# A hybrid decoder layer on one core: a softplus series cut into background pieces, and the mixer's four products in another order

## The chip, the cores and the metric

One core of a Trainium2 chip runs the whole layer. The time is the device time of one execution in microseconds (us). Three runs of the kernel before gave 1193.51, 1194.63 and 1196.12 us, so the median is 1194.63.

## The reference

One layer has three sub-layers on 512 tokens with 1024 channels, in float32. Each one scales and shifts its input by columns that come from a conditioning vector c, adds its result to the residual and normalises. The parts that the change touches are those of the middle sub-layer (`lam` is `rglru_lambda`):

```python
mod = silu(c) @ ada_w + ada_b                  # 9 columns of 1024
u = modulate(x, sh2, sc2)
xr, gr, conf_in, gate_a, gate_b = split(u @ w_in)
xr = causal_depthwise_conv(xr, rnn_conv_w, rnn_conv_b)       # 4 taps
log_a = -8 * softplus(-lam) * sigmoid(xr @ w_r + b_r)        # per head
h  = scan(exp(log_a), sqrt(-expm1(2 * log_a)) * (sigmoid(xr @ w_i + b_i) * xr))
ya = (h * gelu(gr)) @ rnn_w_proj
hb = causal_depthwise_conv(glu(conf_in), conf_dw_w, conf_dw_b)   # 31 taps
yb = silu(layer_norm(hb, conf_ln_g, conf_ln_b)) @ conf_w_proj
out = (sigmoid(gate_a) * ya + sigmoid(gate_b) * yb) @ mix_w_out
```

The first and the third sub-layer are SwiGLU networks with 22 blocks of 128 hidden channels.

## The kernel before

All activations stay in SBUF, channels on the partitions and the 512 tokens along the row; X is the residual. Every product is done in three passes, so that float32 accuracy is kept with a narrower type: an operand is split into a high part (`hi`, a copy into fp32r on ScalarE) and a low part (`lo`, the subtraction, line 145). Weights come in slabs of two blocks of 128 columns (`raw`), and are split in the same way into whi (ScalarE, line 141) and wlo (line 145, on VectorE, or on POOL where `lo_engine` says so). Activations for a product lie in U (Uh, Ul) or in H (Hh, Hl). One block of 128 output channels is a unit: 24 matmuls, 8 chunks of the contraction by 3 passes (lines 240 to 242), into one of six PSUM banks. In the second part of the FFN's contraction a unit has 6 chunks, so 18 matmuls.

The order of work is the order in which the program is written, engine by engine, and each engine works in that order. Three helpers put work between units. `unit()` opens a time slot; weights are split up to four (high) and three (low) units ahead. `defer(n, f)` runs f in the n-th slot from now. `later(cost, f)` puts f in a queue, and `background()`, called twice in a unit, takes pieces from it as long as their costs fit a budget per unit. `until(condition)` holds that queue back until the condition is true. The 31 taps of the depthwise convolution (line 841) are such background work in the mixer, one instruction on VectorE each, and so are the 56 ada sums (line 257) in the first FFN.

The first FFN goes by three parts of hidden blocks: g and u products, h = silu(g) * u, the split of h into H, then eight y products, which add to X (line 714). `early` is called behind the first part's g and u products (`gcol` in `ffn`). It issues the softplus series (lines 939 to 953), which gives the columns sp and nsp for the RG-LRU, and one column for the residual (line 288).

The mixer goes through glu and xr, gr products, with the RG-LRU of each pair of channel blocks deferred behind them; its last step writes the pair's result into H (line 992 and its splits). Then come eight units each of ga, ya, gb and yb. ga and gb read U, ya reads H. `conv_norm` queues the norm over the channels of the convolution's output CV: its sum over the pairs (lc_sum, line 866), a fold of two halves (876), the mean by a matmul (lc_mu, 880), centring (888), squares on ScalarE (890) and their sums (894), the token sums by matmuls (lc_tok, 317), the deviation's power on POOL (334), its diagonal (lc_dg, 341) and broadcast (lc_rs, 908), scaling (914), silu, and the splits into H behind `until(free)`, which is true once the ya products are issued. yb reads H then, and the merged result goes into U.

## Time and profile before

The profiled execution took 1194.8 us, of which 1193.0 us are the span from the first to the last instruction.

| what | value |
|---|---|
| times of three runs | 1193.51, 1194.63, 1196.12 us |
| profiled execution, its span | 1194.8, 1193.0 us |
| mean granted TensorE clock | 0.988 |
| TensorE matmuls, busy | 1159.4 us, 97% |
| VectorE, busy | 747.3 us, 63% |
| ScalarE, busy | 436.6 us, 37% |
| POOL (GpSimd), busy | 215.6 us, 18% |
| DMA | 151.64 MB |

How to read it: PE is TensorE, PEld its weight loads, DVE VectorE, ACT ScalarE, POOL GpSimd, SP the engine that issues the DMAs. A timeline row has the start in us from the span's start, the duration (of several alike, from the first start to the last end), engine, line, operation, output <- inputs, shapes and count; in brackets stands how long the engine was idle before it and what ended the wait. The granted clock is a share of the full 2.4 GHz. Matmuls overlap, so the time of one is the distance from its start to the next one's, and not its duration.

### The profile page before, as it was taken

How to read it: one execution, taken by the hardware profiler on the slowest of the kernel's cores; microseconds unless marked ns; L12 is line 12 of the kernel's file. 1: busy time of each engine (PE TensorE's matmuls, PEld its weight loads, DVE VectorE, ACT ScalarE, POOL GpSimd, SP SyncE). 2: the span in 40 equal slices, each digit the busy share in tenths (PEclk: the TensorE clock that was granted, in tenths of full speed). 3: DMA queues.
4: the chain of work that ended last, by engine and by line, in shares of the span. 5: the costliest groups of instructions: out<-in, count | busy, mean ns of one | idle time of the engine just before them, and what ended most of it. 6: DMA issues, size and time to landing. Idle time of an engine off the chain costs nothing.

```text
span 1193.0 us, 13555 instructions
## 1 busy us (share of the span) xinstructions
PE 1159.4 (97%) x5527; PEld 973.6 (82%) x5527; DVE 747.3 (63%) x1030; ACT 436.6 (37%) x559; POOL 215.6 (18%) x112
## 2 busy tenths in 40 slices
PE   7998999999999999998998999999999999999996
PEld 5887888888889988887787878889888888888886
DVE  7877776733349596998999744587423332433266
ACT  4533222223223625576653372326422122222222
POOL 3200000000003455353536340021400000000002
PEclk9998999999999999998999999999999999999998
DMA  9785766522222122322223212221322222322202
GB/s 372 268 344 207 292 240 230 226 106 105 74 104 107 47 104 80 106 94 78 94 106 116 79 57 102 106 106 36 109 104 107 106 72 79 132 99 79 106 36 71
DMA packets 30318, 151.64 MB, mean 127 GB/s; under 512 B 3376, under 2 KB 5424, under 8 KB 18480
## 3 DMA queue, kind: packets, MB, share of 16 engines
q1 hardware_dynamic: 30256, 150.78, 34.5%
q8 instruction: 43, 0.70, 0.2%
q14 instruction: 19, 0.16, 0.0%
HBM read 148.67 MB, written 2.10 MB: 126 GB/s over the span
## 4 chain that ended last, share of the span: by engine, by line
PE 76%; DVE 15%; issue 4%; ACT 3%; POOL 1%; DMA 1%; SPq 0%; POOLq 0%; ACTq 0%; DVEq 0%
PE g L240 6%; PE u L240 6%; PE u L242 6%; PE g L242 6%; PE g L241 6%; PE u L241 6%; DVE cv L841 6%; PE y L241 6%; PE y L242 6%; PE y L240 6%; PE st L759 4%; DVE i L988 1%; PE yb L240 1%; PE yb L242 1%; PE yb L241 1%
## 5 line engine op out<-in xcount | busy, mean ns | idle before, releaser
L145 POOL TENSOR_TENSOR wlo<-raw,whi 128x1024 fp32r<-128x1024 f32 (+1 forms) x69 | 169.1, 2465 | 568.9 <-ACT whi L141 568.9
L141 ACT CAST whi<-raw 128x1024 fp32r<-128x1024 f32 (+2 forms) x204 | 205.4, 1021 | 165.1 <-DMA raw<-in_wide 124.9
L841 DVE SCALAR_TENSOR_TENSOR cv<-glu,prm,cv 128x511 f32<-128x511 f32 (+14 forms) x240 | 159.4, 728 | 12.5 <-ACT cv L821 12.5
L145 DVE TENSOR_TENSOR wlo<-raw,whi 128x1024 fp32r<-128x1024 f32 (+1 forms) x135 | 158.3, 1191 | 9.2 <-ACT whi L141 9.0
L689 DVE TENSOR_TENSOR h<-u,h 128x512 f32<-128x512 f32 x38 | 26.3, 691 | 205.7 <-PE u L242 205.7
L240 PE MATMUL g<-Uh,whi 128*128 128x512 f32 x304 | 118.3, 389 | 0.0
L241 PE MATMUL g<-Ul,whi 128*128 128x512 f32 x304 | 118.3, 389 | 0.0
L242 PE MATMUL g<-Uh,wlo 128*128 128x512 f32 x304 | 118.3, 389 | 0.0
L240 PE MATMUL u<-Uh,whi 128*128 128x512 f32 x304 | 118.3, 389 | 0.0
L241 PE MATMUL u<-Ul,whi 128*128 128x512 f32 x304 | 118.3, 389 | 0.0
L242 PE MATMUL u<-Uh,wlo 128*128 128x512 f32 x304 | 118.3, 389 | 0.0
L241 PE MATMUL y<-Hl,whi 128*128 128x512 f32 x288 | 113.3, 393 | 3.8 <-DVE Hl L145 3.8
L242 PE MATMUL y<-Hh,wlo 128*128 128x512 f32 x288 | 113.0, 392 | 0.0
L240 PE MATMUL y<-Hh,whi 128*128 128x512 f32 x288 | 113.0, 392 | 0.0
L141 ACT CAST Hh<-h 128x512 fp32r<-128x512 f32 x44 | 27.0, 620 | 178.9 <-DVE h L689 178.9
L257 DVE SCALAR_TENSOR_TENSOR ada<-ada,silu_c 128x1024 f32<-128x1024 f32 x72 | 86.6, 1224 | 5.1 <-DMA ada<-in_ada 5.1
L334 POOL TENSOR_TENSOR l_y<-l_va,half 128x2 f32<-128x2 f32 x5 | 3.5, 708 | 359.1 <-DVE l_va L333 359.1
L241 PEld LDWEIGHTS y<-Hl,whi 128*128 128x128 f32 x288 | 54.7, 190 | 15.7 <-DVE Hl L145 4.2
L242 PEld LDWEIGHTS g<-Uh,wlo 128*128 128x128 f32 x304 | 57.1, 188 | 12.0
L241 PEld LDWEIGHTS u<-Ul,whi 128*128 128x128 f32 x304 | 57.1, 188 | 11.9
L242 PEld LDWEIGHTS u<-Uh,wlo 128*128 128x128 f32 x304 | 57.1, 188 | 11.8
L241 PEld LDWEIGHTS g<-Ul,whi 128*128 128x128 f32 x304 | 57.0, 188 | 11.8
(273 smaller groups left out, 2353.7 us busy)
## 6 DMA issues: line engine op xcount, KB each, us to landing
raw<-in_wide SPq DMA_DIRECT2D x92, 1024.0 KB, 4.8
ada<-in_ada SPq DMA_DIRECT2D x72, 512.0 KB, 7.4
raw<-in_six SPq DMA_DIRECT2D x8, 768.0 KB, 4.2
straw<-in_start SPq DMA_DIRECT2D x8, 512.0 KB, 8.8
X<-in_xT SPq DMA_DIRECT2D x8, 256.0 KB, 9.0
out_y<-X SPq DMA_DIRECT2D x8, 256.0 KB, 2.2
raw<-in_rg SPq DMA_DIRECT2D x4, 256.0 KB, 2.7
silu_c<-in_c SPq DMA_DIRECT2D x1, 512.0 KB, 3.9
```

The lines of the kernel that those rows point to most:

```text
L141: self.nc.scalar.copy(out=out, in_=src)
L145: (engine or self.nc.vector).tensor_tensor(out=out, in0=src, in1=hi.bitcast(F32), op=ALU.subtract)
L240: t.matmul(ps, lhsT=w[0], rhs=x[0], start=first, stop=False)
L241: t.matmul(ps, lhsT=w[0], rhs=x[1], start=False, stop=False)
L242: t.matmul(ps, lhsT=w[1], rhs=x[0], start=False, stop=last)
L257: self.nc.vector.scalar_tensor_tensor(out=raw, in0=raw, scalar=1.0, in1=self.sc, op0=ALU.mult, op1=ALU.mult, accum_out=self.mod[:, j : j + 1])
L334: self.nc.gpsimd.tensor_tensor(out=y, in0=va, in1=self.half[:, :nb], op=ALU.pow)
L689: self.nc.vector.tensor_tensor(out=h, in0=pu, in1=h, op=ALU.mult)
L759: nc.tensor.matmul(ps[i], lhsT=w[k][a][:, i * P : (i + 1) * P], rhs=self.U[b][:, k, :], start=k == 0 and (a, b) == (0, 0), stop=k == KC - ...
L841: self.nc.vector.scalar_tensor_tensor(out=acc[:, n:], in0=glu[:, : T - n], scalar=self.col("conf_dw_w", c, NTAP - 1 - n), in1=acc[:, n:], ...
L988: v.tensor_tensor_scan(out=i_[:, j, :], data0=r[:, j, :], data1=xc[:, j, :], initial=0.0, op0=ALU.mult, op1=ALU.add)
```

## The change

The softplus series is issued after the ada queue, as background pieces: `begin`, `ratio`, eight `term`s and `end`, with costs of 1.0, 1.0, 0.5 each and 1.0. `early` is gone; at its place only the residual's column is computed. In the mixer all sixteen gate products (bank name gate) come first, then ya, then yb, and the slabs of weights lie in that order. The norm's splits write U and not H, and are free once the gate products are issued; yb reads U, the merged result goes to H, and what follows the mixer reads H.

```diff
--- before.py
+++ after.py
@@ -918,9 +918,9 @@
                 nc.scalar.activation(out=x, in_=x, func=AF.Silu, scale=self.col("conf_ln_g", m), bias=self.col("conf_ln_b", m))
 
         def split(p):
-            hi = self.H[0][:, 2 * p : 2 * p + 2, :]
+            hi = self.U[0][:, 2 * p : 2 * p + 2, :]
             self.hi(hi, CV[p])
-            return lambda: self.lo(self.H[1][:, 2 * p : 2 * p + 2, :], CV[p], hi)
+            return lambda: self.lo(self.U[1][:, 2 * p : 2 * p + 2, :], CV[p], hi)
 
         ends = []
         for p in range(4):
@@ -933,24 +933,38 @@
 
     def softplus_cols(self):
 
+
         v, s = self.nc.vector, self.nc.scalar
         lam = self.vec("rglru_lambda")
         sp, nsp, e, z, z2, q = (self.new_drv() for _ in range(6))
-        s.activation(out=e, in_=lam, func=AF.Abs)
-        s.activation(out=e, in_=e, func=AF.Exp, scale=-1.0)
-        v.tensor_scalar(out=z2, in0=e, scalar1=2.0, scalar2=None, op0=ALU.add)
-        v.reciprocal(out=z2, in_=z2)
-        v.tensor_tensor(out=z, in0=e, in1=z2, op=ALU.mult)
-        v.tensor_tensor(out=z2, in0=z, in1=z, op=ALU.mult)
-        v.memset(q, 1.0 / 17)
-        for n in range(15, 0, -2):
+
+        def begin():
+            s.activation(out=e, in_=lam, func=AF.Abs)
+            s.activation(out=e, in_=e, func=AF.Exp, scale=-1.0)
+            v.memset(q, 1.0 / 17)
+
+        def ratio():
+            v.tensor_scalar(out=z2, in0=e, scalar1=2.0, scalar2=None, op0=ALU.add)
+            v.reciprocal(out=z2, in_=z2)
+            v.tensor_tensor(out=z, in0=e, in1=z2, op=ALU.mult)
+            v.tensor_tensor(out=z2, in0=z, in1=z, op=ALU.mult)
+
+        def term(n):
             v.tensor_tensor(out=q, in0=q, in1=z2, op=ALU.mult)
             v.tensor_scalar(out=q, in0=q, scalar1=1.0 / n, scalar2=None, op0=ALU.add)
-        v.scalar_tensor_tensor(out=q, in0=q, scalar=2.0, in1=z, op0=ALU.mult, op1=ALU.mult)
-        v.tensor_scalar(out=z, in0=lam, scalar1=-1.0, scalar2=0.0, op0=ALU.mult, op1=ALU.max)
-        v.tensor_tensor(out=q, in0=q, in1=z, op=ALU.add)
-        v.tensor_scalar(out=sp, in0=q, scalar1=8.0, scalar2=None, op0=ALU.mult)
-        v.tensor_scalar(out=nsp, in0=q, scalar1=-8.0, scalar2=None, op0=ALU.mult)
+
+        def end():
+            v.scalar_tensor_tensor(out=q, in0=q, scalar=2.0, in1=z, op0=ALU.mult, op1=ALU.mult)
+            v.tensor_scalar(out=z, in0=lam, scalar1=-1.0, scalar2=0.0, op0=ALU.mult, op1=ALU.max)
+            v.tensor_tensor(out=q, in0=q, in1=z, op=ALU.add)
+            v.tensor_scalar(out=sp, in0=q, scalar1=8.0, scalar2=None, op0=ALU.mult)
+            v.tensor_scalar(out=nsp, in0=q, scalar1=-8.0, scalar2=None, op0=ALU.mult)
+
+        self.later(1.0, begin)
+        self.later(1.0, ratio)
+        for n in range(15, 0, -2):
+            self.later(0.5, lambda n=n: term(n))
+        self.later(1.0, end)
         return sp, nsp
 
     def rglru(self, mp, xc, gg, rg, sp, nsp):
@@ -1050,49 +1064,45 @@
             for j in range(2):
                 s.activation(out=gg[:, j, :], in_=pg[j], func=AF.Gelu_apprx_tanh)
             self.defer(2, lambda mp=mp, xc=xc, gg=gg, w=self.take(): self.rglru(mp, xc, gg, w, sp, nsp))
-        ya_done = [False]
-        self.conv_norm(lambda: ya_done[0])
+        gates_done = [False]
+        self.conv_norm(lambda: gates_done[0])
 
         self.budget = 4.8
-        ma = [self.pair(f"ma{p}") for p in range(4)]
-        for m in range(KC):
-            ps = self.bank("ga")
-            self.group(ps, self.unit(), self.U)
-            s.activation(out=ma[m // 2][:, m % 2, :], in_=ps, func=AF.Sigmoid)
+        both = []
+        for name in ("ma", "sb"):
+            gates = [self.pair(f"{name}{p}") for p in range(4)]
+            both.append(gates)
+            for m in range(KC):
+                ps = self.bank("gate")
+                self.group(ps, self.unit(), self.U)
+                s.activation(out=gates[m // 2][:, m % 2, :], in_=ps, func=AF.Sigmoid)
+        ma, sb = both
+        gates_done[0] = True
         for m in range(KC):
             ps = self.bank("ya")
             self.group(ps, self.unit(), self.H)
             t = ma[m // 2][:, m % 2, :]
             v.tensor_tensor(out=t, in0=ps, in1=t, op=ALU.mult)
-        ya_done[0] = True
-        sb = [self.pair(f"sb{p}") for p in range(4)]
-        for m in range(KC):
-            ps = self.bank("gb")
-            self.group(ps, self.unit(), self.U)
-            s.activation(out=sb[m // 2][:, m % 2, :], in_=ps, func=AF.Sigmoid)
         self.drain()
         self.lo_engine = nc.vector
         for m in range(KC):
             ps = self.bank("yb")
-            self.group(ps, self.unit(), self.H)
+            self.group(ps, self.unit(), self.U)
             t = sb[m // 2][:, m % 2, :]
             v.tensor_tensor(out=t, in0=ps, in1=t, op=ALU.mult)
             v.tensor_tensor(out=t, in0=t, in1=ma[m // 2][:, m % 2, :], op=ALU.add)
-            hi = self.U[0][:, m, :]
+            hi = self.H[0][:, m, :]
             self.hi(hi, t)
-            self.defer(1, lambda m=m, t=t, hi=hi: self.lo(self.U[1][:, m, :], t, hi))
-        self.ln_front("l2", self.U, g)
+            self.defer(1, lambda m=m, t=t, hi=hi: self.lo(self.H[1][:, m, :], t, hi))
+        self.ln_front("l2", self.H, g)
 
     def run(self):
         nc, d, X = self.nc, self.d, self.X
-        def early():
-            self.softplus = self.softplus_cols()
-            return self.gate_col(G1, 0.5)
-
         self.startup()
         self.ada_queue()
+        self.softplus = self.softplus_cols()
         self.budget = 2.0
-        g1 = self.ffn("l1", 4, early)
+        g1 = self.ffn("l1", 4, lambda: self.gate_col(G1, 0.5))
         self.drain()
         c2 = self.affine_cols("ln1_g", "ln1_b", SC2, SH2)
         hb = self.boundary("l1", self.H, g1, c2)
@@ -1100,7 +1110,7 @@
         self.mixer(hb, g2, c2)
         c3 = self.affine_cols("ln2_g", "ln2_b", SC3, SH3)
         self.budget = 0.0
-        hb = self.boundary("l2", self.U, g2, c3)
+        hb = self.boundary("l2", self.H, g2, c3)
         ends = [self.swiglu(hb[2 * i], hb[2 * i + 1], i) for i in range(2)]
         for e in ends:
             e()
@@ -1162,8 +1172,8 @@
         order.append(("rg", mp, [4 * P]))
         rg.append(np.concatenate([w[2 * mp + j] for w in (wr, wi) for j in range(2)], axis=1))
     both(ga)
+    both(gb)
     both(i["rnn_w_proj"])
-    both(gb)
     both(i["conf_w_proj"])
     both(i["mix_w_out"])
     ffn(2, 0)
```

The first place is VectorE at the end of the first part of the first FFN, where h is the last hidden block, drv are the small columns, and Hl is the low part of that block, which the y products read. Before:

```order
L689 TENSOR_TENSOR h_776<-u,h_776 128x512
L941 TENSOR_SCALAR drv<-drv 128x8
L942 RECIPROCAL drv<-drv 128x8
...
L952 TENSOR_SCALAR drv<-drv 128x8
L953 TENSOR_SCALAR drv<-drv 128x8
L288 TENSOR_SCALAR drv<-mod 128x8
L145 TENSOR_TENSOR Hl<-h_776,Hh 128x512
```

and now:

```order
L689 TENSOR_TENSOR h_776<-u,h_776 128x512
L288 TENSOR_SCALAR drv<-mod 128x8
L145 TENSOR_TENSOR Hl<-h_776,Hh 128x512
```

The 26 instructions of the series no longer stand between h and Hl. They now stand among the y products of the second part, on the same engine (X<-y adds a product to the residual):

```order
L278 TENSOR_TENSOR mod<-mod,prm 128x8
L944 MEMSET drv 128x8
L714 SCALAR_TENSOR_TENSOR X<-y,drv,X 128x512
L145 TENSOR_TENSOR wlo_1684<-raw_1566,whi_1651 128x768
L947 TENSOR_SCALAR drv<-drv 128x8
L948 RECIPROCAL drv<-drv 128x8
...
L954 TENSOR_SCALAR drv<-drv 128x8
L714 SCALAR_TENSOR_TENSOR X<-y,drv,X 128x512
```

The rest follows behind the next two additions to X, eight and eleven instructions at a time.

The second place is TensorE in the mixer, from the last ga product to the first yb product. Before:

```order
L242 MATMUL ga<-Uh,wlo_4443 128x512
L240 MATMUL ya<-Hh,whi_4441 128x512
...
L242 MATMUL ya<-Hh,wlo_4761 128x512
L240 MATMUL gb<-Uh,whi_4759 128x512
...
L880 MATMUL lc_mu<-lc_sum,inv_d 128x512
...
L242 MATMUL gb<-Uh,wlo_5060 128x512
L240 MATMUL yb<-Hh,whi_5058 128x512
```

and now:

```order
L242 MATMUL gate<-Uh,wlo_4443 128x512
L240 MATMUL gate<-Uh,whi_4441 128x512
...
L242 MATMUL gate<-Uh,wlo_4765 128x512
L240 MATMUL ya<-Hh,whi_4763 128x512
...
L880 MATMUL lc_mu<-lc_sum,inv_d 128x512
...
L242 MATMUL ya<-Hh,wlo_5060 128x512
L240 MATMUL yb<-Uh,whi_5058 128x512
```

The first ya product changed places with the first gb product, and the matmuls of the norm's statistics stand at the same rows, now between ya products.

The third place is VectorE in the norm, from the fold of lc_sum to the token sums (ma<-ya multiplies a ya product by its gate and so frees its bank). Before:

```order
L1066 TENSOR_TENSOR ma_4245<-ya,ma_4245 128x512
L876 TENSOR_TENSOR lc_sum<-lc_sum 128x512
L1066 TENSOR_TENSOR ma_4246<-ya,ma_4246 128x512 x2
L888 TENSOR_TENSOR CV_3442<-CV_3442,lc_mu 128x1024
L888 TENSOR_TENSOR CV_3999<-CV_3999,lc_mu 128x1024
L894 TENSOR_TENSOR lc_q_4924<-lc_q_4924,lc_q_4927 128x1024
L888 TENSOR_TENSOR CV_4486<-CV_4486,lc_mu 128x1024
...
L894 TENSOR_TENSOR lc_q_4924<-lc_q_4924,lc_q_4965 128x1024
L876 TENSOR_TENSOR lc_q_4924<-lc_q_4924 128x512
L327 TENSOR_SCALAR lc_va<-lc_tok 128x4
```

and now:

```order
L866 TENSOR_TENSOR lc_sum<-lc_sum,CV_4821 128x1024
L876 TENSOR_TENSOR lc_sum<-lc_sum 128x512
L888 TENSOR_TENSOR CV_3442<-CV_3442,lc_mu 128x1024
L888 TENSOR_TENSOR CV_3999<-CV_3999,lc_mu 128x1024
L894 TENSOR_TENSOR lc_q_4924<-lc_q_4924,lc_q_4927 128x1024
L1085 TENSOR_TENSOR ma_4243<-ya,ma_4243 128x512
L888 TENSOR_TENSOR CV_4486<-CV_4486,lc_mu 128x1024
...
L894 TENSOR_TENSOR lc_q_4924<-lc_q_4924,lc_q_4965 128x1024
L1085 TENSOR_TENSOR ma_4243<-ya,ma_4243 128x512
L876 TENSOR_TENSOR lc_q_4924<-lc_q_4924 128x512
L1085 TENSOR_TENSOR ma_4244<-ya,ma_4244 128x512
```

The ya evacuations, of which six stood ahead of the fold and two right behind it, now stand among the norm's own instructions, three of them ahead of the one that reads lc_tok, and five behind it.

## Rows read from the trace of the kernel before

**Rows 1.** The profile's page, part 1: busy time, share of span, instructions by engine.

```profile
PE 1159.4 (97%) x5527; PEld 973.6 (82%) x5527; DVE 747.3 (63%) x1030; ACT 436.6 (37%) x559; POOL 215.6 (18%) x112
```

**Rows 2.** Waits of TensorE: us in total, times, longest.

```profile
PE y L241 <- DVE Hl L145: 3.8, 1, 3.8
PE ya L241 <- DVE Hl L145: 3.4, 1, 3.4
```

**Rows 3.** Two stretches: busy us of each engine, granted clock, DMA share.

```profile
103.80:113.88 10.08, 6.25 (x16) 4.63 (x15) 9.53 (x29) 0.37 (x1) 0.00 (x0) 0.66 0.34 124
627.28:636.19 8.91, 5.55 (x18) 4.07 (x16) 8.91 (x14) 3.82 (x6) 8.81 (x4) 0.81 0.20 66
```

**Rows 4.** Timeline of TensorE at y: start, us, operation, idle before.

```profile
99.04 0.39 PE L240 MATMUL y<-Hh,whi 128*128 128x512 f32 x1
103.80 0.39 PE L240 MATMUL y<-Hh,whi 128*128 128x512 f32 x1
...
108.01 0.80 PE L241 MATMUL y<-Hl,whi 128*128 128x512 f32 x1 [3.83 <-DVE Hl L145]
...
113.88 0.39 PE L240 MATMUL y<-Hh,whi 128*128 128x512 f32 x1
```

**Rows 5.** Timeline of VectorE at the series.

```profile
99.31 0.69 DVE L689 TENSOR_TENSOR h<-u,h 128x512 f32<-128x512 f32 x1 [1.96 <-PE u L242]
102.32 0.17 DVE L941 TENSOR_SCALAR drv<-drv 128x8 f32<-128x8 f32 x1 [2.32 <-ACT drv L940]
...
107.28 0.68 DVE L145 TENSOR_TENSOR Hl<-h,Hh 128x512 fp32r<-128x512 f32 x1
```

**Rows 6.** Timeline of ScalarE there.

```profile
100.03 0.62 ACT L141 CAST Hh<-h 128x512 fp32r<-128x512 f32 x1 [4.70 <-DVE h L689]
...
100.78 1.28 ACT L940 ACT_TABLE_LOAD   x1
```

**Rows 7.** Timeline of TensorE at ya.

```profile
627.28 0.39 PE L240 MATMUL ya<-Hh,whi 128*128 128x512 f32 x1
...
636.19 0.39 PE L241 MATMUL ya<-Hl,whi 128*128 128x512 f32 x1
```

**Rows 8.** Timeline of VectorE, last taps to the sum's fold.

```profile
629.77 1.21 DVE L145 TENSOR_TENSOR Hl<-i,Hh 128x1024 fp32r<-128x1024 f32 x1
...
640.63 0.68 DVE L1066 TENSOR_TENSOR ma<-ya,ma 128x512 f32<-128x512 f32 x1
641.23 4.58 DVE L841 SCALAR_TENSOR_TENSOR cv<-glu,prm,cv 128x498 f32<-128x498 f32 x7
...
667.70 2.30 DVE L876 TENSOR_TENSOR lc_sum<-lc_sum 128x512 f32<-128x512 f32 x1
```

**Rows 9.** Timeline of POOL.

```profile
627.38 10.55 POOL L145 TENSOR_TENSOR wlo<-raw,whi 128x1024 fp32r<-128x1024 f32 x4 [12.05 <-ACT whi L141]
...
680.73 2.40 POOL L145 TENSOR_TENSOR wlo<-raw,whi 128x1024 fp32r<-128x1024 f32 x1 [6.12 <-ACT whi L141]
688.00 2.73 POOL L145 TENSOR_TENSOR wlo<-raw,whi 128x1024 fp32r<-128x1024 f32 x1 [4.87 <-ACT whi L141]
```

**Rows 10.** Timeline of TensorE, statistics of the convolution's norm.

```profile
674.73 1.02 PE L880 MATMUL lc_mu<-lc_sum,inv_d 128*128 128x512 f32 x2
...
691.95 0.95 PE L317 MATMUL lc_tok<-inv_d,lc_q 128*128 128x1 f32 x8
...
697.21 1.10 PE L908 MATMUL lc_rs<-lc_dg,ones 128*128 128x512 f32 x2 [1.43 <-DVE lc_dg L341]
```

**Rows 11.** Timeline of VectorE, the norm.

```profile
687.79 0.69 DVE L876 TENSOR_TENSOR lc_q<-lc_q 128x512 f32<-128x512 f32 x1
...
694.21 2.85 DVE L341 TENSOR_TENSOR lc_dg<-prm,lc_y 128x512 f32<-128x512 f32 x1 [1.12 <-POOL lc_y L334]
...
706.33 4.63 DVE L145 TENSOR_TENSOR Hl<-CV,Hh 128x1024 fp32r<-128x1024 f32 x4 [3.37 <-ACT Hh L141]
```

**Rows 12.** Timeline of VectorE, y products of the second FFN part.

```profile
239.21 0.75 DVE L714 SCALAR_TENSOR_TENSOR X<-y,drv,X 128x512 f32<-128x512 f32 x1 [2.20 <-PE y L242]
```

## The prediction

> **What bounds the kernel now.** I read the busy times first: TensorE's matmuls stand for 97% of the span and VectorE's work for 63% [rows 1]. So I looked for TensorE's own waits, and then for what each of them is made of. The list of waits by engine names two that fall on operands which the change touches: the y products waited once for Hl (3.8 us), and the ya products once for Hl (3.4 us) [rows 2]. The stretches around these two show what they cost in all: in 103.80 to 113.88 us TensorE issued 16 matmuls at a mean granted clock of 0.66, in 627.28 to 636.19 us 18 at 0.81 [rows 3]. After each wait the clock stands at the lower of its two levels (1.2 GHz) for some us before it is back at 2.4.
>
> **What a wait costs, step by step.** Undisturbed, 21 matmuls go from 99.04 to 103.80 us, 0.2267 us each [rows 4], so a product of 24 takes 5.44 us. First place: from 103.80 to 113.88 there are 15 issues, which would take 3.40 us and took 10.08; lost 6.68 us, 3.98 of it the gap (4.21 less 0.23) and 2.70 the slow clock behind it [rows 4]. Second place: from 627.28 to 636.19 there are 16 issues, 3.63 us, that took 8.91; lost 5.28 us [rows 7].
>
> **The change part by part.** *The softplus series.* On VectorE 26 small instructions stood between the last h of the first FFN part and the Hl that the y products read. VectorE stood still from 100.0 to 102.32 for ScalarE's table load and Exp, ran the series, and came to Hl at 107.28; TensorE needed it from 104.03 [rows 4 to 6]. They now stand behind the ada sums, among the y products of the second part. At the old place only one column instruction stays between h and Hl. Hh is done at 100.65 [rows 6], so Hl can run at 100.7 and end at 101.4, 2.6 us before TensorE asks. The whole 6.68 us go. At the new place VectorE idles about 2.2 us in each product's 4.08 us (18 matmuls) [rows 12]; the pieces are 1, 6, 8 and 11 instructions there, and with the old spacing, 4.96 us from the first to Hl over 27 instructions or 0.18 us each [rows 5], 0.2 to 2.0 us. Each fits in one idle stretch, and weights are split three units ahead of use; I cost it at 0. Without that cover a whole series would be 4.9 us late, against a lead of two to three products (8 to 12 us), so 0 at the other end too. The Abs and Exp, with their table load of 1.28 us [rows 6], move with it. ScalarE loads the Silu table again behind it as it did before; two table loads less in the mixer are off the path.
>
> *The order of products.* The wait at 627 us was for the Hl of the last RG-LRU pair, which VectorE, busy with convolution taps, delivered at 631.0 [rows 7, 8]. Eight gb products, which read U, now stand at this place. ya comes eight products later. By its 19th matmul at 627.28, ya began at 623.2. With the 5.28 us gone gb fills 623.2 to 666.7, and ya begins 36 us after its operand is there. What is late next? The first POOL split of the four from 627.38 [rows 9] serves the third product from 623.2 on (the series of weight units is unchanged). It ends near 630.0; TensorE wants it at 634.1. So 5.28 us go.
>
> *The norm of the convolution under ya instead of gb.* TensorE arrives at the mean's matmul 5.28 us sooner, at 669.45 in this frame instead of 674.73 [rows 10]. Its operand was ready at 670.0 [rows 8]. But six ya evacuations leave VectorE's queue ahead of it (five among the taps, one between the sum and the fold), 0.60 us each from start to next start [rows 8], so it is ready at 666.4, with 3.0 us to spare. From there to lc_tok the two programs keep the same distance on TensorE. On VectorE two evacuations are added, 1.2 us; the fold ended at 688.48 and lc_tok began at 691.95 [rows 10, 11], so 2.3 us of cover stay. lc_rs waits 1.43 us for lc_dg [rows 10]; the instructions of that stretch are the same, so I keep it at 1.43. Bounds: it could vanish (minus 1.4) or be hit by one more POOL split (plus 2.4). Behind it one evacuation lies within the wait for lc_rs and one between the first two lo splits; those ended at 710.96 [rows 11], and yb began near 720.0 (lc_rs from 697.21 to about 698.3, then 96 gb matmuls at 0.2267 us [rows 10]), 9.0 us later. 1.2 us more leave 7.8. ScalarE evacuated gb and VectorE evacuates ya; with six banks TensorE comes back to ya's first bank 5 products (27 us) after filling it, and VectorE gets there within about 2 us (behind one lc_q sum). 0 us.
>
> *The other buffers.* The normed operand goes to U after the last gate product has read it, the merged one to H after ya: the waits on these reads are past by 8 products, 0 us. sb now lives beside the convolution outputs, so lc_q1 to lc_q3 and lc_dg share one buffer. Each write then waits for a VectorE sum that already stands ahead of it in the chain: 0 us, and at most a sum's 1.2 us each within the 2.3 us above.
>
> At the fold the trace speaks against a free passage: two VectorE instructions on two SBUF operands took 2.30 and 2.85 us where POOL ran a split at their side, against 0.69 us for the same fold without one [rows 8, 9, 11]. The Trainium skill, page "SBUF — State Buffer", section "SBUF: two separate sides", has it that VectorE (with two SBUF inputs) and GpSimd share a port pair as an exclusive lock, and that the loser blocks for the whole instruction of the other; the rows agree. By that rule and by the new order one more collision is due here, worked out next from rows alone.
>
> With a ya evacuation between the last lc_q sum and the fold, VectorE leaves a gap of 0.60 us in which the POOL split of 688.00 can start (before, it started as the fold ended) [rows 9, 11]. The fold then runs behind 2.4 us of POOL work: 2.27 us of cover less 2.4 is a wait of 0.1 us. I take 0 and keep 2.4 as the end of the range.
>
> **Sum.** The profiled execution took 1194.8 us (span 1193.0 and 1.8 around it), 0.2 over the median of the three. 1194.8 less 6.68 less 5.28 is 1182.8 us, minus 1.0%.
>
> **Rivals.** (B) *The norm's chain becomes a wait at lc_tok.* For it: the cover of 2.27 us, and two collisions of 2.4 us each exceed it by 2.5, which with a slow clock behind (up to 1.9 us, the second place's 5.28 less its wait of 3.4) gives 1185.3 to 1187.2. Against it: POOL started only two splits between lc_mu and lc_tok, and the first ran clear of the sums [rows 9]. (C) *Only one of the two waits goes*, since another operand is late behind it: 1188.1 (only the first goes) or 1189.5 (only the second). For it: VectorE is busy for all of the second stretch (8.91 of 8.91 us) [rows 3]. Against it: the margins of 2.6 and 4.1 us above. (D) *VectorE's queue takes over as the bound under ya, slower than before.* Place: the chain from the mean to the lo splits, with eight evacuations in it. It decides if POOL's splits block every sum: four at 2.4 us ahead of lc_tok (9.6, less 2.3 of cover, plus 2.7 of slow clock as at the first place, 10.0), and four lo splits (9.6 plus 1.2, less the 9.0 us before yb, plus 2.7, 4.5): 14.5 us, so 1197.3. Against it: that many splits don't lie there. (E) *The change does not do what it says*, as the series delays another Hl or weights at its new place and gives the 6.7 back, and gb meets an equal wait: within 0.2% of 1194.8.
>
> **Chances.** Forecast 0.80, B 0.09, C 0.06, D 0.02, E 0.03. Own range of the forecast: 1181.0 (lc_rs no longer waits) to 1185. The range, 1180.8 to 1187.5, takes in B and the bounds, and leaves out C, D and E. A measurement of this kernel tells about 0.2% (2.4 us) from no change: faster 0.95 (forecast, B and C), same 0.03 (E), slower 0.02 (D).
>
> **What would show it.** Right: no wait of TensorE for Hl at y or at ya in the list of waits, granted clock 1.0 in the slices around 104 and 630 us, mean and lc_tok without a wait, lc_rs with about 1.4 us, and the wait of the first xr/cb stage as it was, 6.7 us earlier. The forecast is wrong if TensorE waits over 1 us at lc_mu or lc_tok, at a gate product for a split, at yb for Ul, or at a y product of the second part.

## The result

| kernel | median, us | runs, us | number of runs |
|---|---|---|---|
| before, beside it | 1194.07 | 1193.51 to 1196.12 | 4 |
| changed | 1182.95 | 1182.42 to 1185.17 | 4 |

The ratio is 0.9908, with an interval of 0.9893 to 0.9924: 1% faster. 1182.8 us had been forecast. The profiled executions took 1194.8 us (before) and 1182.73 (changed), a difference of 12.07 us where the sum had 11.96. That they agree so closely is in part luck: both executions came to their first y product after 99.0 us, and others with the same code took up to 100.6.

### The profile page after: what moved, and what is told of

Its sections match the earlier page's. It is cut to its first block, busy times and chain, and to the rows that moved or that the text cites. A ratio compares the mean times of both kernels' runs of the same rounds, so it can differ in the third digit from the quotient of the medians.

```text
span 1180.9 us, 13555 instructions
## 1 busy us (share of the span) xinstructions
PE 1154.6 (98%) x5527; PEld 970.4 (82%) x5527; DVE 749.1 (63%) x1030; ACT 434.0 (37%) x557; POOL 216.6 (18%) x112
## 4 chain that ended last, share of the span: by engine, by line
PE 83%; DVE 9%; issue 3%; ACT 2%; POOL 1%; DMA 1%; SPq 0%; POOLq 0%; ACTq 0%; DVEq 0%
PE g L240 6%; PE u L240 6%; PE g L242 6%; PE u L242 6%; PE g L241 6%; PE u L241 6%; PE y L240 6%; PE y L241 6%; PE y L242 6%; PE st L759 4%; PE gate L240 2%; PE gate L242 2%; PE gate L241 2%; DVE cv L841 2%; PE yb L241 1%
## 5 line engine op out<-in xcount | busy, mean ns | idle before, releaser
L241 PE MATMUL y<-Hl,whi 128*128 128x512 f32 x320 | 124.5, 389 | 0.0
L242 PE MATMUL y<-Hh,wlo 128*128 128x512 f32 x320 | 124.5, 389 | 0.0
L240 PE MATMUL y<-Hh,whi 128*128 128x512 f32 x320 | 124.5, 389 | 0.0
L242 PEld LDWEIGHTS y<-Hh,wlo 128*128 128x128 f32 x320 | 60.1, 188 | 12.5
L240 PEld LDWEIGHTS y<-Hh,whi 128*128 128x128 f32 x320 | 60.1, 188 | 12.5
L241 PEld LDWEIGHTS y<-Hl,whi 128*128 128x128 f32 x320 | 60.1, 188 | 12.5
L685 ACT ACTIVATE h<-g 128x512 f32<-128x512 f32 x38 | 22.7, 597 | 120.4 <-PE g L242 120.4
L242 PEld LDWEIGHTS g<-Uh,wlo 128*128 128x128 f32 x304 | 57.1, 188 | 11.9
```

Source lines behind the costliest of these rows:

```text
L240: t.matmul(ps, lhsT=w[0], rhs=x[0], start=first, stop=False)
L241: t.matmul(ps, lhsT=w[0], rhs=x[1], start=False, stop=False)
L242: t.matmul(ps, lhsT=w[1], rhs=x[0], start=False, stop=last)
L685: self.nc.scalar.activation(out=h, in_=pg, func=AF.Silu)
```

## The profile after

The changed kernel's page, part 1, and its list of TensorE's waits (us in total, times, longest):

```profile
PE 1154.6 (98%) x5527; PEld 970.4 (82%) x5527; DVE 749.1 (63%) x1030; ACT 434.0 (37%) x557; POOL 216.6 (18%) x112
```

```profile
PE cb L240 <- DVE xc L1053: 3.5, 1, 3.5
PE lc_rs L908 <- DVE lc_dg L341: 1.4, 1, 1.4
...
PE gate L240 <- ACT ma L1078: 0.7, 1, 0.7
```

Both waits of [rows 2] are gone, and none has appeared at y, ya, lc_mu or lc_tok. The stretches at their places, the second 6.75 us earlier on the clock (columns as in [rows 3]):

```profile
103.80:113.88 10.08, 10.08 (x46) 8.37 (x45) 7.96 (x12) 2.11 (x2) 0.00 (x0) 1.00 0.70 267
620.53:629.44 8.91, 8.91 (x41) 7.39 (x40) 8.91 (x14) 4.89 (x7) 8.84 (x4) 1.00 0.20 64
```

TensorE works through both at the full clock, 46 and 41 matmuls where there were 16 and 18. In the second one VectorE is busy to the last and POOL for 8.84 us, as before; only TensorE no longer waits for them.

To see where time goes without adding up waits, I cut the execution at instructions that both kernels have: the first y product, the first l1t (the matmuls at the end of the first FFN), the first cb (a product of the glu), the end of the wait at the third product of the gates (ga before), the first yb. Rows of the changed kernel's timeline of TensorE:

```profile
99.01 0.39 PE L240 MATMUL y<-Hh,whi 128*128 128x512 f32 x1
...
349.49 0.28 PE L240 MATMUL l1t<-Hh,whi 128*128 128x256 f32 x1
...
402.21 0.40 PE L240 MATMUL cb<-Uh,whi 128*128 128x512 f32 x1
...
544.59 0.76 PE L240 MATMUL cb<-Uh,whi 128*128 128x512 f32 x1 [3.47 <-DVE xc L1053]
583.61 0.50 PE L240 MATMUL gate<-Uh,whi 128*128 128x512 f32 x1 [0.66 <-ACT ma L1078]
...
707.84 0.39 PE L240 MATMUL yb<-Uh,whi 128*128 128x512 f32 x1
```

The first four columns of this table are differences of two starts, for the profiled execution of each kernel (experiments below); the last two show what stood behind the wait at cb, and how long the gates waited:

| kernel | start to y | y to l1t | cb to gates' wait | gates' wait to yb | slow issues behind cb's wait | wait at the gates |
|---|---|---|---|---|---|---|
| before | 99.04 | 257.18 | 181.43 | 129.56 | 12 | 0.63 |
| changed | 99.01 | 250.48 | 181.40 | 124.23 | 12 | 0.66 |
| changed, again | 100.55 | 250.49 | 181.41 | 124.24 | 6 | 1.93 |
| series only | 100.60 | 250.49 | 181.39 | 129.52 | 12 | 0.66 |
| order only | 99.65 | 256.23 | 181.40 | 125.84 | 5 | 2.08 |
| one gb first | 100.50 | 250.49 | 181.41 | 125.84 | 5 | 2.04 |
| Exp early | 100.36 | 252.18 | 181.43 | 130.79 | 7 | 1.81 |
| rs later | 100.29 | 250.48 | 181.44 | 122.57 | 8 | 1.81 |
| sums sooner | 100.38 | 250.48 | 181.41 | 126.18 | 12 | 0.75 |
| sums sooner, joined | 99.06 | 250.49 | 181.40 | 126.19 | 7 | 1.82 |

A slow issue is a matmul at whose side the next one starts 0.427 us later instead of 0.227. From yb to the last pair of matmuls (l_rs) before and after are alike (464.55 and 464.56). So the change took 6.70 us between y and l1t, and 5.33 between the gates and yb, and elsewhere no more than 0.03 in any stretch.

The gates' wait ends 181.39 to 181.44 us after the first cb in all ten. ScalarE's queue and VectorE's show what it hangs on (changed kernel):

```profile
577.46 1.21 DVE L1006 TENSOR_TENSOR i<-i,gg 128x1024 f32<-128x1024 f32 x1
...
578.70 1.05 ACT L141 CAST Hh<-i 128x1024 fp32r<-128x1024 f32 x1 [8.71 <-DVE i L1006]
...
582.96 0.60 ACT L1078 ACTIVATE ma<-gate 128x512 f32<-128x512 f32 x1
```

ma, for which the third product of the gates waits, stands in ScalarE's queue behind an Hh that waits for the last step of an RG-LRU on VectorE, two weight copies and a table load. Between the ends of TensorE's two waits VectorE (the third column of work) is busy for 35.98 of 39.02 us, and for 35.99 of 39.03 when the changed kernel ran again with half as many slow issues there:

```profile
544.59:583.61 39.02, 38.37 (x156) 31.15 (x156) 35.98 (x42) 24.16 (x30) 15.18 (x7) 0.93 0.23 82
```

```profile
546.15:585.18 39.03, 37.10 (x156) 30.25 (x156) 35.99 (x42) 24.05 (x30) 15.17 (x7) 0.96 0.23 82
```

So VectorE sets the pace of this stretch, and TensorE's clock doesn't.

**The norm under ya.** VectorE in the changed kernel, from the mean's operand to the last split (timeline):

```profile
657.45 0.69 DVE L876 TENSOR_TENSOR lc_sum<-lc_sum 128x512 f32<-128x512 f32 x1
...
674.91 1.23 DVE L894 TENSOR_TENSOR lc_q<-lc_q,lc_q 128x1024 f32<-128x1024 f32 x1 [1.19 <-ACT lc_q L890]
676.05 0.69 DVE L1085 TENSOR_TENSOR ma<-ya,ma 128x512 f32<-128x512 f32 x1
676.65 2.30 DVE L876 TENSOR_TENSOR lc_q<-lc_q 128x512 f32<-128x512 f32 x1
...
695.99 5.70 DVE L145 TENSOR_TENSOR Ul<-CV,Uh 128x1024 fp32r<-128x1024 f32 x3
```

and TensorE and POOL at the fold:

```profile
662.63 1.02 PE L880 MATMUL lc_mu<-lc_sum,inv_d 128*128 128x512 f32 x2
...
679.86 0.95 PE L317 MATMUL lc_tok<-inv_d,lc_q 128*128 128x1 f32 x8
...
685.12 1.10 PE L908 MATMUL lc_rs<-lc_dg,ones 128*128 128x512 f32 x2 [1.43 <-DVE lc_dg L341]
```

```profile
657.67 7.45 POOL L145 TENSOR_TENSOR wlo<-raw,whi 128x1024 fp32r<-128x1024 f32 x3 [9.87 <-ACT whi L141]
...
675.89 2.50 POOL L145 TENSOR_TENSOR wlo<-raw,whi 128x1024 fp32r<-128x1024 f32 x1 [5.17 <-ACT whi L141]
```

The fold does meet the POOL split and takes 2.30 us, as had been feared, against 0.69 in [rows 11]. It ends at 678.95, and lc_tok begins at 679.86 without a wait: 0.91 us of cover are left of the 3.47 that stood between fold and lc_tok before (688.48 to 691.95). The mean's operand is ready at 658.14, 4.5 us ahead of lc_mu.

## The experiments

The kernels were timed beside the kernel before on the same chip, in three groups; its medians there were 1194.92 us (the first four), 1194.92 (the next four) and 1194.85 (the last three).

**Series only.** The kernel before with the series as background pieces, as in the changed kernel (that part of the edit is left out here); the mixer is as before.

```diff
...
+        self.softplus = self.softplus_cols()
         self.budget = 2.0
-        g1 = self.ffn("l1", 4, early)
+        g1 = self.ffn("l1", 4, lambda: self.gate_col(G1, 0.5))
```

> The kernel before with the softplus series in background pieces, and nothing else changed. Theory (each of the two waits for Hl is paid for by itself, wait plus slow clock behind it): the wait at y and its slow stretch go, 6.7 us, ratio 0.9944, about 1187.4 us; the wait of ya for Hl stays at 3.4 us with a clock below 1.0 behind it. Rival (the series only moves its cost): under 2 us of gain, and a wait at a y product of the second part.

Measured: 1189.37 us (1187.77 to 1189.58, 5 runs), ratio 0.9948 [0.9934, 0.9962]. That is 2.0 us more than expected, and 1.56 of it lies at the start of the profiled execution (100.60). The wait at y is gone, and from y to l1t it takes what the changed kernel takes, 250.49 us. The other wait stays, and the stretch from gates to yb with it (129.52):

```profile
PE ya L241 <- DVE Hl L145: 3.3, 1, 3.3
```

**Order only.** The changed kernel with the series at its old place, in one piece (`early` issues the series, then the column; the rest of the edit is left out here).

```diff
...
-        self.softplus = self.softplus_cols()
         self.budget = 2.0
-        g1 = self.ffn("l1", 4, lambda: self.gate_col(G1, 0.5))
+        g1 = self.ffn("l1", 4, early)
```

> The changed kernel with the softplus series back at its old place. Theory: only the 5.3 us of the second place go, ratio 0.9956, about 1188.8 us; the wait at y is 3.8 us again. Rival (the two waits hang together, since an earlier stretch sets VectorE's lag in the mixer): a gain clearly other than 5.3 us.

Measured: 1189.85 us (1189.79 to 1193.09, 5 runs), ratio 0.9965 [0.9952, 0.9977]; the expected 0.9956 lies in the interval. Its waits are the mirror of the kernel before:

```profile
PE y L241 <- DVE Hl L145: 3.8, 1, 3.8
...
PE gate L240 <- ACT ma L1064: 2.1, 1, 2.1
```

The stretch from gates to yb is 1.61 us longer than in the changed kernel, since 7 slow issues (7 x 0.2 us, and two at 0.38 and 0.28) follow the gates' wait here. From y to l1t it takes 256.23 us, 0.95 less than the kernel before: the wait is as long (3.81 us), but 7 slow issues follow it and not 11. Each half of the change acts alone and at its own place: rivals C and E fall.

**One gb first.** Only one gb product stands between ga and ya, seven behind it; the norm's operand is back in H. So the order is 8 ga, 1 gb, 8 ya, 7 gb (cut to the lines that set it).

```diff
...
-        for name in ("ma", "sb"):
...
+        gate_b(0)
         for m in range(KC):
             ps = self.bank("ya")
...
```

> Series in background pieces as in the changed kernel; in the mixer the order is ga (8), one gb, ya (8), gb (7), yb, and the buffers H and U as in the kernel before. Theory (the second place is worth its lateness alone: Hl comes 3.5 us late, one product is 5.4 us): the wait of ya for Hl is gone, and nearly all of the 5.3 us with it, 1183 to 1184.5 us (the mean's operand comes just in time here, so up to 1 us of wait at lc_mu). Rival (it takes the other buffer pair, or ScalarE free of gates during the norm): about 1188 us.

Measured: 1184.93 us (1184.26 to 1185.82, 4 runs), ratio 0.9917 [0.9904, 0.9931]. No wait at ya. By the table its profiled execution (1185.82) lies 3.09 us over that of the changed kernel for two reasons that have nothing to do with the order: 1.49 us at the start and 1.61 behind the gates' wait, which 8 slow issues follow. So the Hl of the last pair needs one product's delay; eight are more than it takes. Moving the norm under ya brought nothing of its own that these stretches show: order only, which has it there and about as many slow issues behind the gates' wait, takes the same 125.84 us from that wait to yb.

**Exp early.** The kernel before, with Abs and Exp issued some products earlier; the series itself stays between h and Hl. One run.

```diff
...
+        def begin():
+            nc.scalar.activation(out=e, in_=lam, func=AF.Abs)
+            nc.scalar.activation(out=e, in_=e, func=AF.Exp, scale=-1.0)
...
+        self.later(0.0, begin)
         self.ada_queue()
```

> The kernel before with only Abs and Exp (and their table load) of the series issued earlier, in the background queue; the 26 VectorE instructions stay between h and Hl. Theory: VectorE need not stand still for Exp, the series runs from 100.0 to 104.8 us, Hl ends near 105.5, and TensorE, which wants it at 104.0, waits 1.3 to 1.6 us; such a short wait brings no slow clock (as the 1.43 us wait at lc_rs brought none), so the first place costs about 1.5 us in place of 6.7, and the run is about 1189.3 us. Rival (any wait here drops the clock): 1.5 plus 2.7 us, about 1192 us, and a granted clock below 1.0 between 104 and 114 us.

Measured: 1192.32 us, 3.0 more than expected. VectorE no longer stands still for ScalarE's table, and Hl begins 5.55 us after h (100.63, 106.18), 2.42 less than the 7.97 of [rows 5]. The wait at y shrinks, and nothing slow follows it:

```profile
PE y L241 <- DVE Hl L145: 1.4, 1, 1.4
```

```profile
104.00:114.00 10.00, 8.59 (x38) 6.82 (x37) 9.66 (x26) 1.11 (x2) 0.00 (x0) 1.00 0.48 177
```

y to l1t takes 252.18 us, 1.70 over a kernel without a wait there, so 5.0 of the 6.7 us are won by the earlier Abs and Exp alone. The total is that of the rival, but its sign, a clock below 1.0 there, is missing. The miss lies elsewhere in that one execution: 1.32 us at the start, and 1.23 between gates and yb, where 13 slow issues follow the wait at ya instead of 7; the 1189.3 was also 0.3 less than its own terms give (1194.8 less 6.68 plus 1.5).

**rs later.** The changed kernel with lc_rs half a product later.

```diff
-            self.quick.append((0, bc))
+            self.quick.append((1, bc))
```

> The changed kernel with lc_rs (the matmul that spreads the norm's scale) put half a product, 2.72 us, later in TensorE's order. In the changed kernel it waits 1.43 us for lc_dg. Theory (the time is that of TensorE's own waits): the wait goes and nothing comes in its place, since the lo splits behind lc_rs end 5.6 us before yb begins: 1182.7 less 1.4 is 1181.3 us (1180.8 to 1181.8). Rival (VectorE's queue sets the end of this stage): lc_rs's later place makes Ul late and yb waits; 1182.7 or more.

Measured: 1182.49 us (1182.37 to 1184.13, 4 runs), ratio 0.99 [0.9886, 0.9913]. The wait at lc_rs is gone, and gates to yb falls from 124.23 to 122.57 us, by 1.66 where 1.4 were due; yb does not wait. In the total, which lies over the expected range, it is hidden: its profiled execution began y 1.28 us later. The totals don't tell it from the changed kernel.

**Sums sooner**, and **sums sooner, joined.** lc_tok half a product sooner; in the second kernel the fold is also issued in one piece with the last sum.

```diff
-LC_MEAN, LC_SUMS = 4, 2
+LC_MEAN, LC_SUMS = 4, 1
```

```diff
+        def add(p):
+            v.tensor_tensor(out=st["q0"], in0=st["q0"], in1=st[f"q{p}"], op=ALU.add)
+            if p == 3:
+                self.credit -= 0.6
+                fold(st["q0"])
...
-        self.later(0.6, lambda: fold(st["q0"]))
```

> The changed kernel with lc_tok half a product, 2.72 us, sooner in TensorE's order. In the changed kernel the fold that lc_tok reads ends at 678.95 us (it ran 2.30 us beside a POOL split) and lc_tok begins at 679.86, so 0.9 us of cover are left of the 2.27 that the prediction began with. Theory: lc_tok would now be reached at about 677.1, 1.8 us before its operand: a wait of about 1.8 us, with no slow clock or a short one behind it: 1184.5 us (1184.0 to 1186.0), lc_rs's wait unchanged. Rival (the collision at the fold is harmless, there is more cover than this): 1182.7.

> The same as the kernel before it (lc_tok 2.72 us sooner), and the fold joined to the last lc_q sum, so that VectorE issues them back to back and no POOL split can start between them. Theory (the fold's 2.30 us against 0.69 come from the split that runs at its side): the fold takes 0.69 us and ends near 676.8, lc_tok at 677.1 does not wait: 1182.7 us (1182.2 to 1183.3), 1.8 less than the kernel before it. Rival (the split would block VectorE wherever it falls, so that the sum in front of the fold takes the delay instead): the wait at lc_tok stays at 1 us or more, 1184 or more.

Measured: 1186.08 us (1185.52 to 1186.19, 5 runs; ratio 0.9927 [0.9913, 0.9941]) and 1185.55 (1184.75 to 1186.36, 4 runs; 0.9922 [0.9909, 0.9936]). The first waits 1.69 us at lc_tok, as expected: the cover was 0.9 us and no more. Its lc_rs, which was to wait as before, doesn't, and its time is 0.1 us over the expected range. Joining the fold did not help; the expectation fell to its rival in the time, though not in the way: the sum took its 1.23 us, and the fold the delay. TensorE in the first of them, then in the second:

```profile
680.37 1.05 PE L317 MATMUL lc_tok<-inv_d,lc_q 128*128 128x1 f32 x8 [1.69 <-DVE lc_q L876]
...
682.21 0.63 PE L242 MATMUL ya<-Hh,wlo 128*128 128x512 f32 x1
682.64 0.63 PE L240 MATMUL ya<-Hh,whi 128*128 128x512 f32 x1
...
685.73 1.10 PE L908 MATMUL lc_rs<-lc_dg,ones 128*128 128x512 f32 x2
```

```profile
679.05 1.05 PE L317 MATMUL lc_tok<-inv_d,lc_q 128*128 128x1 f32 x8 [1.68 <-DVE lc_q L876]
...
684.43 1.10 PE L913 MATMUL lc_rs<-lc_dg,ones 128*128 128x512 f32 x2 [1.45 <-DVE lc_dg L341]
```

VectorE and POOL in the second:

```profile
674.99 1.23 DVE L892 TENSOR_TENSOR lc_q<-lc_q,lc_q 128x1024 f32<-128x1024 f32 x1 [1.19 <-ACT lc_q L890]
676.25 2.75 DVE L876 TENSOR_TENSOR lc_q<-lc_q 128x512 f32<-128x512 f32 x1
```

```profile
675.97 2.48 POOL L145 TENSOR_TENSOR wlo<-raw,whi 128x1024 fp32r<-128x1024 f32 x1 [5.17 <-ACT whi L141]
```

Two things are to be seen. With no instruction of VectorE between sum and fold, the split still gets in: it begins 0.28 us before the fold, as the sum ends. And in the first kernel the wait at lc_tok is followed by 7 slow issues, in the second by none; but there lc_rs waits 1.45 us and in the first it doesn't. Gates to yb is 126.18 and 126.19 us. The slow clock cost nothing in the sum where the next operand would have been late anyway.

**No cb wait.** An attempt at the largest wait left in the mixer, cb at 544.59.

```diff
-        for n, fn in enumerate((a, b, c, e)):
-            self.defer(n + 2, fn)
+        for n, fn in zip((2, 3, 4, 6), (a, b, c, e)):
+            self.defer(n, fn)
...
-        self.budget = 3.2
+        self.budget = 2.9
...
-        self.budget = 4.8
+        self.budget = 5.4
```

The first budget is that of the four xr/cb stages, the second that of the gates.

> The changed kernel, and the one wait of TensorE over 2 us that is left in its mixer taken on: cb at 544.6 us waits 3.47 us for VectorE's xc taps, with 12 slow issues (2.4 us) behind it, 5.9 us in all. Two edits: the background budget 2.9 instead of 3.2 in the xr/cb stages and 5.4 instead of 4.8 under the gates (about two convolution taps fewer per stage, done later), and the RG-LRU's last product (L1006) with its Hh and Hl one half product later, so that ScalarE's xc no longer stands behind an Hh that waits for it. Theory (TensorE's waits make the time, and a wait of 2 us or less is followed by little slow clock): the wait falls to about 0.3 us; of the 5.9 us some 1 to 1.5 come back as a longer wait at the first gate, where VectorE is late by about 0.7 us already: 1178.3 us (1177.0 to 1180.0). Rival (VectorE's work in the mixer is the bound, the wait only stands where it shows): the same lag appears at the gates, ya or lc_mu: 1181.5 to 1184.

Measured: 1208.83 us (1207.39 to 1209.45, 4 runs), ratio 1.0115 [1.0102, 1.0129]. Theory and rival both miss. cb now waits twice:

```profile
PE cb L240 <- DVE xc L1053: 9.8, 2, 6.5
...
PE lc_mu L880 <- DVE lc_sum L876: 3.5, 1, 3.5
```

ScalarE shows why:

```profile
499.49 0.77 ACT L1049 ACTIVATE xc<-xr,prm 128x512 f32<-128x512 f32 x1
512.16 1.04 ACT L141 CAST Hh<-i 128x1024 fp32r<-128x1024 f32 x1 [11.90 <-DVE i L1006]
513.22 1.28 ACT L983 ACT_TABLE_LOAD   x1
```

The moved Hh no longer stands in front of xc, but in front of the r and i of the next pair and the xc behind them, and ScalarE stands still for 11.9 us at its head. The wait for L1006 was moved from one victim to another. How much of the loss is the budget's and how much the move's was not taken apart.

**Taps sooner**, and **taps sooner, rs later.** Another way to the same end: only the taps are spread otherwise over the four xr/cb stages.

```diff
-        self.budget = 3.2
         for mp in range(4):
+            self.budget = (4.4, 3.2, 2.6, 3.2)[mp]
```

> The changed kernel with the convolution taps of the xr/cb stages spread otherwise over the four stages: background budget 4.4, 3.2, 2.6, 3.2 instead of 3.2 in each, so 11 taps more in the first stage (VectorE stood idle 6.3 of 11 us there, 456 to 467 us) and 5 fewer, with their 3.3 us, before the xc of the fourth, where cb waits 3.47 us. Nothing else moves. Theory (TensorE's waits make the time): the wait at cb falls to under 1 us, and its 12 slow issues with it: 5.9 us less there. TensorE then comes sooner to the first gate, whose wait grows from 0.7 to about 2: 1182.7 less 5.9 plus 1.3 is 1178.1 us (1177 to 1180). Rival (VectorE's work up to the gates is the bound, the wait only stands where it first shows): the gate's wait takes it all back, 1182 to 1184; or VectorE's added taps delay a Hl or a bank in the first stage, over 1184.

> The kernel before it, with lc_rs 2.72 us later besides. That step took the stretch from lc_mu to yb from 45.21 to 43.55 us when it was tried alone, 1.66 us. Theory: it adds up, 1178.1 less 1.7 is 1176.4 us (1175 to 1179). Rival (what is saved at one place comes back at the next wait): no less than the kernel before it.

Measured: 1187.01 us as the median of four runs (1186.46 to 1187.65; ratio 0.9937 [0.9923, 0.995]; a fifth took 4430.44 us at a mean granted clock of 0.252, for a reason that isn't known, and is left out) and 1186.42 (1185.67 to 1187.77, 5 runs; 0.9933 [0.992, 0.9945]). The wait at cb is gone, and one product sooner there is another (TensorE, then ScalarE, in the first of the two):

```profile
540.42 0.80 PE L240 MATMUL ri<-Hh,whi 128*128 128x512 f32 x1 [4.25 <-ACT gg L1065]
```

```profile
536.54 0.58 ACT L846 COPY CV<-cv 128x512 f32<-128x512 f32 x1 [8.96 <-DVE cv L841]
```

A convolution now ends in this stage, and its copy stands in ScalarE's queue ahead of gg. The gates' wait ends at 586.40, 183.03 us after the first cb, 1.6 us more than in the kernels of the table. So nothing is won there: the gates' wait takes it back, as the rival had it. Its time of 1182 to 1184 is missed too, since 1.15 us lie at the start (100.16) and 2.13 more between the gates' wait and yb (126.36). lc_mu came half a product sooner in TensorE's order, and lc_tok then waited 1.9 us for its fold (beside a split, 2.75 us again). lc_rs later took 1.5 us from yb's start (712.76 to 711.35, with 0.1 more at the start), where it had taken 1.66 alone: that step adds up, on a kernel that is 9 us slower than was expected.

**Changed, again.** The changed kernel without an edit, on the chip of the last two.

> The changed kernel as it is, on the same chip as the two before it. 1182.7 us (1182.4 to 1185.2, as its four runs); its profile tells whether the length of the start-up (l1t began between 349.5 and 350.9 us in the profiles of kernels with the same code there) and of the slow clock after the cb wait of 3.47 us (5 to 12 slow issues so far) belong to a kernel or to an execution. Theory: to an execution, so one of them differs here from the first profile of the same kernel (start-up 349.49, 12 slow issues). Rival: both come out the same again.

Measured: 1183.44 us (1182.62 to 1184.29, 4 runs), ratio 0.9904 [0.9889, 0.9919]. The start was 1.54 us longer (1184.29 us for the profiled execution, against 1182.73), and the wait at cb was followed by 6 slow issues, not 12. The granted clock of the 8 us behind cb's wait, in the first profile and in this one:

```profile
544.59:552.59 8.00, 8.00 (x23) 6.36 (x24) 5.51 (x8) 5.88 (x9) 2.40 (x1) 0.63 0.01 2
```

```profile
546.15:554.15 8.00, 8.00 (x29) 6.48 (x30) 5.51 (x8) 5.88 (x9) 2.40 (x1) 0.80 0.01 2
```

So both can differ between two executions of one kernel. The six issues less gave nothing:

```profile
585.18 0.50 PE L240 MATMUL gate<-Uh,whi 128*128 128x512 f32 x1 [1.93 <-ACT ma L1078]
```

The gates' wait is longer by what the clock had saved (1.93 for 0.66), and ends 181.41 us after the first cb, as in every kernel of the table.

## Why the prediction was right

**The series (6.68 predicted, 6.70 measured).** Hl at y ended at 101.35 (predicted 101.4), and y to l1t alone, with the series only, shrank by 6.69. The zero at the new place holds, with as little room as the prediction's own numbers gave (a piece of 2.0 us in 2.2 us of idle time): the last piece, 11 instructions, ran from 234.29 to 236.35, and VectorE had 0.22 us left before the next X (Hl at its old place first, then that X):

```profile
100.66 0.69 DVE L145 TENSOR_TENSOR Hl<-h,Hh 128x512 fp32r<-128x512 f32 x1 [0.61 <-ACT Hh L141]
...
236.57 0.75 DVE L714 SCALAR_TENSOR_TENSOR X<-y,drv,X 128x512 f32<-128x512 f32 x1 [0.22 <-PE y L242]
```

**The order (5.28 predicted, 5.33 measured).** Shown by the order alone and by one gb in front of ya. The xr/cb stage waits its 3.47 us as before, 6.75 us earlier; it is the fourth of these stages (551.34 before, 544.59 now), and not the first, as the prediction had it.

**How far the sizes agree.** Each predicted size was read from the same execution of the kernel before that the measured one is taken against, so that an agreement to 0.05 us says that nothing else moved, and not that a place always costs this. By the profile of order only the wait at y costs 5.74 us (256.23 less 250.49); by those of series only and Exp early the wait at ya costs 5.29 and 6.56 (129.52 and 130.79 less 124.23). The waits are alike, the slow issues behind them are not.

**The mean's operand (3.0 us early predicted, 4.5 measured).** The evacuations left its chain as counted. The fold in [rows 8] had run 2.30 us, which the prediction carried over. There a POOL split had begun 0.75 us ahead of it:

```profile
666.95 7.66 POOL L145 TENSOR_TENSOR wlo<-raw,whi 128x1024 fp32r<-128x1024 f32 x3 [13.15 <-ACT whi L141]
```

In the changed kernel the split began 0.22 us behind the fold (657.67, 657.45), and the fold took 0.69. That is 1.6 us, and about the 1.5 that were missed.

**The fold before lc_tok (a wait of 0.1 us or none; none, with 0.91 to spare).** That a collision was due there was right; its size wasn't. A whole split of 2.4 us was charged, but the split had run for 0.76 us when the fold came, and the fold lost 1.61 (2.30 for 0.69). The evacuations and the rest of the chain cost 0.96 where 1.2 were charged. 3.47 less 2.57 is the 0.90 found. The prediction read the split of 688.00 as starting when the fold ended, and it had started 0.21 us after the fold began (687.79), without slowing it. The reason given, that an evacuation between sum and fold lets the split in, is not needed: without it (sums sooner, joined) the split got in as well. What decides is which of the two comes first. Over thirteen profiles the fold took 0.69 us in the four where it began 0.2 us before the split (before, series only, one gb first, Exp early) and 2.27 to 2.78 in the nine where the split began 0.27 to 0.76 before it. The split took 2.73 to 2.75 us in the four, and 2.47 to 2.51 in the nine. The fold of lc_sum in the same thirteen is the mirror: 2.29 to 2.30 us in those four, where a split began 0.74 to 0.75 before it, and 0.69 in the nine, where it began 0.22 behind. The Trainium skill, page "SBUF — State Buffer", section "SBUF: two separate sides", says so of the port pair that GpSimd and VectorE (with two SBUF inputs) share: whichever starts first gets it for the whole instruction. The rows agree, and that half of the rule is the one that the prediction should have used.

**lc_rs (1.43 kept; 1.43 found)** and **Ul (7.8 us before yb predicted, 6.15 found).** The splits met one more POOL split: three Ul in 5.70 us. Still far from yb.

**The rivals.** C and E fall by the halves run alone. The prediction held against B that the split of 680.73 ran clear of the sums; it didn't quite, since the sum of 682.75 took 1.47 us at its end, where the next took 1.23. B came within 0.9 us of happening, as the sums put half a product sooner show, with 1.96 us as the price of a wait of 1.7 (126.19 less 124.23). D's place showed three collisions (the fold, lc_dg as before, one Ul), not eight.

**What the sum took for granted.** Wait and slow clock were both counted as lost. At y and ya that was right, since nothing waits for several products behind them. It is not a property of the wait: behind cb's wait 12 slow issues, 2.4 us by the same counting, are worth nothing, as 5, 6, 7 and 8 of them gave the same end. So a prediction of 5.9 us for cb by the method used here would have been wrong by at least these 2.4, and mine for the two attempts at it were wrong by more. What the gap of 3.47 us is worth by itself is not shown: both attempts moved other work too, and brought waits of their own.

## What to carry to other kernels

Price a wait by the stretch up to the next operand or bank that another engine delivers, and not by the gap and the slow clock behind it: if that is only just in time, what is saved is waited for there. A late operand was mended here by putting other TensorE work in front of its reader; both attempts to move work on the late engine instead moved what stood at the head of a third engine's queue, and with it the wait. And compare kernels by stretches between instructions that they share: differences of 0.1 us are seen there, while totals of one kernel lie 2 to 3 us apart.

## What the runs showed of the hardware

- The slow clock behind equal waits is not equally long. After 3.44 to 3.48 us at cb there were 5 to 12 slow issues in ten profiles, with the same code around it. Of five waits of 2.04 to 2.08 us at the gates three were followed by 7 or 8 (order only, one gb first, no cb wait) and two by none; at lc_tok one of 1.69 by 7, one of 1.68 by none.
- The start, up to the first y, takes 99.0 to 100.6 us with the same code; the same kernel showed 99.01 and 100.55. The wait of the first statistics for ScalarE, 5.4 to 6.4 us, goes with it and is up to 1.0 us of the difference; the rest was not looked into.
